# Second layer's feed-forward: gate and up by one level of Strassen in token halves of 512

## The chip, the cores and the metric

The kernel runs on one core of one Trainium2 chip. The metric is the device time of one execution in microseconds (us). Runs of this kernel lie within some 0.15% of each other.

## What is computed

A decoder trunk of two layers, for 1024 tokens and 16 meta tokens in front of them (1040), model width 1024, in float32. Each layer is a token mixer and a gated feed-forward block (SwiGLU) with 2816 hidden features; the change is in what follows the second layer's attention.

```python
for i in range(DEPTH):
    hn = rms_norm(h, mix_norm_g[i])
    ...
    h = h + swiglu(rms_norm(h, ffn_norm_g[i]), ffn_w_gate[i], ffn_w_up[i], ffn_w_down[i])
h = rms_norm(h, final_norm_g)
return h[:, N_META:]

def swiglu(h, w_gate, w_up, w_down):
    return (jax.nn.silu(h @ w_gate) * (h @ w_up)) @ w_down
```

## The kernel before

**Matrix products.** Activations lie with the features on the 128 partitions and the tokens along the free axis. Each float32 operand is split into a high part, rounded by ScalarE (a CAST in the profile), and a low part, the rest, subtracted by VectorE or GpSimd (`split_w` L153, `norm_gen` L261). A product is then three TensorE matmuls (`mm3`, L163 to L165: high by high, high by low, low by high) into one PSUM bank; the fourth, low by low, is left out.

**Tokens.** They are handled in three chunks of 348, 348 and 344; in the second layer the meta tokens are dropped, and the chunks are 332, 348 and 344 wide. The residual `h` lies in SBUF during a feed-forward block and in the DRAM tensor `hdram` during attention.

**Feed-forward** (`ffn`). The 2816 features are 22 tiles of 128, taken in 11 pairs. For each tile and chunk `phase_a` makes gate and up (8 blocks of the contraction, 24 matmuls each) in a PSUM pair `gu`; ScalarE applies SiLU (L549), VectorE multiplies (L551), and the product is split into `ah` and `al`. For each chunk `phase_b` multiplies by the pair's down weights into 8 banks `y`, which VectorE adds to `h` (L567). A pair is 2 x 3 x 48 = 288 matmuls for gate and up and 3 x 8 x 6 = 144 for down, 432 in all, of 332 to 348 columns. The weights of a tile (`raw_g`, `raw_u`, `raw_d`, 512 KB each) come by SyncE's DMA queue and are split in whole tiles, 128 x 1024.

**Around it.** The attention's output projection is made in pieces: `wo_early_gen` for the chunk of 332 during the last heads, `wo_part` and `wo_gen` for the other two, `wo_last` for the last head's share (`wot`). `wo_tail` weaves these with the three norms of the feed-forward's input, `norm_gen` (squares on ScalarE, sums `acc_f` on GpSimd, two small matmuls for the statistics, then `xt_f`, `xh_f`, `xl_f` for each of 8 blocks). The last pair is woven with the final norm (`final` in `run`), and its last chunk (332 tokens) is in hand-written order. Elsewhere a scheduler orders each engine's instructions from the program's order and its estimates.

## Time and profile before

| | us |
|---|---|
| three runs | 2196.35, 2196.79, 2199.15 (median 2196.79) |
| the profiled execution, its own time | 2194.79 |
| its span | 2193.0 |
| TensorE busy | 2158.8 |
| VectorE, ScalarE, GpSimd busy | 1065.3, 726.0, 354.8 |

PE is TensorE, DVE VectorE, ACT ScalarE, POOL GpSimd, SP SyncE, whose queue issues all DMAs. The profile gives for each group of instructions its busy time, its mean duration and what ended the idle time of its engine just before. Matmul durations overlap in it; the distance between two starts is what one costs in a row. PEclk is the granted clock of TensorE, 1.00 for 2.4 GHz and 0.50 for 1.2 GHz.

### The profile page before, as it was taken

How to read it: one execution, taken by the hardware profiler on the slowest of the kernel's cores; microseconds unless marked ns; L12 is line 12 of the kernel's file. 1: busy time of each engine (PE TensorE's matmuls, PEld its weight loads, DVE VectorE, ACT ScalarE, POOL GpSimd, SP SyncE). 2: the span in 40 equal slices, each digit the busy share in tenths (PEclk: the TensorE clock that was granted, in tenths of full speed). 3: DMA queues.
4: the chain of work that ended last, by engine and by line, in shares of the span. 5: the costliest groups of instructions: out<-in, count | busy, mean ns of one | idle time of the engine just before them, and what ended most of it. 6: DMA issues, size and time to landing. Idle time of an engine off the chain costs nothing.

```text
span 2193.0 us, 33618 instructions
## 1 busy us (share of the span) xinstructions
PE 2158.8 (98%) x13978; PEld 2141.7 (98%) x13978; DVE 1065.3 (49%) x2000; ACT 726.0 (33%) x1509; POOL 354.8 (16%) x542
## 2 busy tenths in 40 slices
PE   8999999999999999999999999999999999999998
PEld 7999999999999999999999999999999999999998
DVE  6653334343343446777666677464343333333335
ACT  5531211112111134666666655242112211112114
POOL 4300000000000025444444333230000000000004
PEclk8999999999999999999999999999999999999998
DMA  7011101011110112111111147212011111111002
...
DMA packets 49363, 137.02 MB, mean 62 GB/s; under 512 B 5346, under 2 KB 20491, under 8 KB 48699
## 3 DMA queue, kind: packets, MB, share of 16 engines
...
q14 instruction: 43, 0.35, 0.0%
...
## 4 chain that ended last, share of the span: by engine, by line
PE 92%; DVE 3%; ACT 3%; DMA 1%; issue 1%; POOL 0%; SPq 0%; DVEq 0%; ACTq 0%; POOLq 0%
PE gu L163 15%; PE gu L164 15%; PE gu L165 15%; PE y L163 7%; PE y L164 7%; PE y L165 7%; PE pj L165 4%; PE pj L163 4%; PE pj L164 4%; PE o L880 2%; PE s L800 2%; PE o L885 1%; PE at L863 1%; PE s L798 1%; PE pl L353 1%; DVE xt_f L258 1%
## 5 line engine op out<-in xcount | busy, mean ns | idle before, releaser
L567 DVE TENSOR_TENSOR h<-h,y 128x348 f32<-128x348 f32 (+2 forms) x520 | 263.0, 511 | 315.3 <-PE y L165 315.1
L549 ACT ACTIVATE s<-gu 128x348 f32<-128x348 f32 (+1 forms) x132 | 60.2, 456 | 831.3 <-PE gu L165 831.2
L163 PE MATMUL y<-ah,d_h 128*128 128x348 f32 (+2 forms) x1008 | 321.6, 321 | 3.8 <-DVE h L567 3.6
L164 PE MATMUL y<-al,d_h 128*128 128x348 f32 (+2 forms) x1008 | 322.4, 320 | 0.0
L165 PE MATMUL y<-ah,d_l 128*128 128x348 f32 (+2 forms) x1008 | 322.4, 320 | 0.0
L164 PE MATMUL gu<-xl_f,u_h 128*128 128x348 f32 (+2 forms) x1008 | 321.9, 319 | 0.0
L164 PE MATMUL gu<-xl_f,g_h 128*128 128x348 f32 (+2 forms) x1008 | 321.7, 319 | 0.0
L165 PE MATMUL gu<-xh_f,u_l 128*128 128x348 f32 (+2 forms) x1008 | 321.6, 319 | 0.1
L163 PE MATMUL gu<-xh_f,g_h 128*128 128x348 f32 (+2 forms) x1008 | 321.7, 319 | 0.0
L165 PE MATMUL gu<-xh_f,g_l 128*128 128x348 f32 (+2 forms) x1008 | 321.6, 319 | 0.0
L163 PE MATMUL gu<-xh_f,u_h 128*128 128x348 f32 (+2 forms) x1008 | 321.5, 319 | 0.0
L551 DVE TENSOR_TENSOR s<-gu,s 128x348 f32<-128x348 f32 (+1 forms) x132 | 67.9, 514 | 346.1 <-ACT s L549 346.1
L163 PEld LDWEIGHTS y<-ah,d_h 128*128 128x128 f32 x1008 | 190.0, 189 | 5.7 <-DVE h L567 5.3
L164 PEld LDWEIGHTS y<-al,d_h 128*128 128x128 f32 x1008 | 190.6, 189 | 0.0
L165 PEld LDWEIGHTS y<-ah,d_l 128*128 128x128 f32 x1008 | 190.1, 189 | 0.0
L164 PEld LDWEIGHTS gu<-xl_f,g_h 128*128 128x128 f32 x1008 | 189.5, 188 | 0.6 <-issue 0.6
L165 PEld LDWEIGHTS gu<-xh_f,u_l 128*128 128x128 f32 x1008 | 189.6, 188 | 0.3 <-DVE u_l L153 0.3
L163 PEld LDWEIGHTS gu<-xh_f,g_h 128*128 128x128 f32 x1008 | 189.6, 188 | 0.0
L165 PEld LDWEIGHTS gu<-xh_f,g_l 128*128 128x128 f32 x1008 | 189.6, 188 | 0.0
L163 PEld LDWEIGHTS gu<-xh_f,u_h 128*128 128x128 f32 x1008 | 189.6, 188 | 0.0
L164 PEld LDWEIGHTS gu<-xl_f,u_h 128*128 128x128 f32 x1008 | 189.5, 188 | 0.0
L163 PE MATMUL pj<-xh_m,w_h 128*128 128x348 f32 (+2 forms) x576 | 187.9, 326 | 0.9 <-DVE oo L922 0.9
...
## 6 DMA issues: line engine op xcount, KB each, us to landing
...
```

The lines of the kernel that those rows point to most:

```text
L163: nc.tensor.matmul(out, wh, xh, start=first, stop=False)
L164: nc.tensor.matmul(out, wh, xl, start=False, stop=False)
L165: nc.tensor.matmul(out, wl, xh, start=False, stop=last)
L258: nc.vector.scalar_tensor_tensor(t[:, :w], h[:, k, a:b], self.gcol(g, k), r[:, :w], op0=ALU.mult, op1=ALU.mult)
L353: yield lambda x=x, i=i: self.nc.tensor.matmul(ps[:, a:b], x[:r, j, k * P : k * P + P], rhs, start=start and i == 0, stop=stop and i == 1)
L549: nc.scalar.activation(st[:, :w], ps[:, 0, :w], AF.Silu)
L551: nc.vector.tensor_tensor(at[:, :w], ps[:, 1, :w], st[:, :w], op=ALU.mult)
L567: nc.vector.tensor_tensor(h[:, m, a:b], h[:, m, a:b], ps[:, :w], op=ALU.add)
L798: nc.tensor.matmul(out, qz[m], s["kl"][:, ka:kb], start=False, stop=True)
L800: nc.tensor.matmul(out, s["qs", m][:, qsl], s["kd", m][:, ka:kb], start=True, stop=False)
L863: nc.tensor.transpose(pt[:rows, j, :], a[:, kb * KB : kb * KB + rows], self.ident)
L880: nc.tensor.matmul(po[:, : 2 * P], ah[:rows, kb, :], s["vhl"][:rows, kb, :], start=j == 0, stop=j == nl)
```

## The change

`layer1` takes the place of `wo_tail` and of the second layer's `ffn`. Tokens are handled in two halves of 512, and `h` becomes one tile `H` (128 x 8 x 1024). The first and the last pair of features are computed as before, but 512 columns wide (the last chunks 512, 256, 256). For the nine pairs between (`wino`), gate and up are 2 x 2 block products: a pair's two feature tiles by two token halves, with the contraction of 1024 in two halves. Winograd's form of Strassen's scheme does each with seven products instead of eight.

- The four sums of weight blocks S1 to S4 (tiles `z`) are made by GpSimd for each pair and projection (`sub`, 8 instructions a pair). The sums of token blocks T1 to T4 are made once (`twist_gen`): VectorE and GpSimd add and subtract the split parts, and the sums are split anew. T4 takes the place of a block of x and is turned back before the last pair.
- Each product has 12 matmuls of 512 columns. Its weights are a `unit`, split from 128 x 512 by ScalarE and VectorE into one of five buffers (`ring`).
- Products 6, 4 and 5 are added in PSUM onto banks that hold earlier ones, and between these ScalarE copies a bank out (`hold`) and VectorE adds another to the copy (`put`).
- `down_gen` multiplies the pair before by its down weights, 96 matmuls of 512 columns.

A Strassen pair thus has 2 x 84 + 96 = 264 matmuls of 512 columns. Beside them stand 14 splits of units, 8 holds, 8 puts, 4 SiLU, 4 multiplications, 4 splits of activations, 4 splits of down weights and 16 additions to `H`.

```diff
...
+HALF = 512
+OFF1 = {1: 0, 2: 512, 0: 768}
+W1 = {1: 512, 2: 256, 0: 256}
+NT = 6
+NRING = 5
...
+    def wo_last(self, ox, wr):
...
+                self.mm3(ps, ww, [self.part8(ox, hl, NH - 2 + j) for hl in range(2)], j == js[0], j == 1)
+            nc.vector.tensor_tensor(h[:, m, :], h[:, m, :], ps, op=ALU.add)
...
+    def split(self, src, hi, lo, eng=None):
+        self.nc.scalar.copy(hi, src)
+        (eng or self.nc.vector).tensor_tensor(lo, src, hi.bitcast(F32), op=ALU.subtract)
+
+    def unit(self, src, nm, pool=None, tag="u", eng=None, f2=False):
+        t = (pool or self.ring).tile([P, 2, HALF], F32R, tag=tag, name=nm)
+        hi, lo = t[:, 0, :], t[:, 1, :]
+        if f2:
+            self.split(src, *(v.rearrange("p (f n) -> p f n", f=2) for v in (hi, lo)), eng)
+        else:
+            self.split(src, hi, lo, eng)
+        return hi, lo
+
...
+        def diff(nm, a, b, op=ALU.subtract):
+            d, e = self.tt(f"{nm}d"), self.tt(f"{nm}e")
+            V.tensor_tensor(d, a[0], b[0], op=op)
+            G.tensor_tensor(e, a[1], b[1], op=op)
+            V.tensor_tensor(d, d, e, op=ALU.add)
+            return d
+
+        def less(nm, a, b):
+            d = self.tt(f"{nm}d")
+            V.tensor_tensor(d, a[0], b, op=ALU.subtract)
+            V.tensor_tensor(d, d, a[1], op=ALU.add)
+            return d
+
...
+        def pair(n, k):
+            return [self.T[n, hl, k] for hl in range(2)]
+
+        for k in range(4):
+            b11, b12, b21, b22 = ([part(j, i, hl, k) for hl in range(2)] for i in range(2) for j in range(2))
+            t3 = diff(f"t3_{k}", b22, b12)
+            self.split(t3, *pair(3, k), G)
+            t1 = diff(f"t1_{k}", b12, b11)
+            self.split(t1, *pair(1, k), G)
+            t2 = less(f"t2_{k}", b22, t1)
+            self.split(t2, *pair(2, k), V)
+            yield
+        yield True
+        for k in range(4):
+            t4 = diff(f"t4_{k}", [part(0, 1, hl, k) for hl in range(2)], [t.bitcast(F32) for t in pair(2, k)])
+            self.split(t4, *pair(4, k), V)
+        yield True
+        for k in range(4):
+            b12 = diff(f"b12_{k}", [part(0, 0, hl, k) for hl in range(2)], [t.bitcast(F32) for t in pair(1, k)], ALU.add)
+            self.split(b12, *pair(4, k), G)
+
...
+    def wino(self, p, nm, src, x, use):
+        nc, ap = self.nc, self.ap
+        V, G = nc.vector, nc.gpsimd
+        held = {}
+
+        def hold(i, j, b):
+            if nm == "u" and i == j == 1:
+                t = self.actp.tile([P, HALF], F32, tag="ex", name=f"c{nm}_{p}_{i}{j}")
+            else:
+                t = self.tt(f"c{nm}_{p}_{i}{j}")
+            held[i, j] = t
+            nc.scalar.copy(t, b)
+
+        def put(i, j, b):
+            t = held.pop((i, j))
+            V.tensor_tensor(t, t, b, op=ALU.add)
+            use(i, j, t)
+
+        raw = self.raw2([ap[src][FT + 2 * p + i] for i in range(2)], f"raw_{nm}_{p}")
+        A = {(i + 1, k + 1): raw[:, i, k * HALF : k * HALF + HALF] for i in range(2) for k in range(2)}
+        S = dict(enumerate(self.z, 1))
+
+        def sub(o, a, b, op=ALU.subtract):
+            G.tensor_tensor(S[o], a, b, op=op)
+
+        xw = self.psa(f"xw_{nm}_{p}")
+        X, W = xw[:, 0, :], xw[:, 1, :]
+
+        def mul(out, n, a, b, start=True):
+            hi, lo = self.unit(a, f"w{n}_{nm}_{p}")
+            for k in range(4):
+                ww = [t[:, k * P : k * P + P] for t in (hi, lo)]
+                self.mm3(out, ww, [b(hl, k) for hl in range(2)], start and k == 0, k == 3, skip=not start)
+
+        def bx(i, j):
+            return lambda hl, k: self.part8(x[j], hl, 4 * i + k)
+
+        def bt(n):
+            return lambda hl, k: self.T[n, hl, k]
+
+        sub(3, A[1, 1], A[2, 1])
+        sub(1, A[2, 1], A[2, 2], ALU.add)
+        mul(X, 1, A[1, 1], bx(0, 0))
+        yield
+        Y = self.psb(f"y2_{nm}_{p}")
+        mul(Y, 2, A[1, 2], bx(1, 0))
+        hold(0, 0, Y)
+        put(0, 0, X)
+        yield
+        mul(W, 7, S[3], bt(3))
+        hold(1, 1, W)
+        sub(2, S[1], A[1, 1])
+        sub(4, A[1, 2], S[2])
+        yield
+        mul(X, 6, S[2], bt(2), False)
+        yield
+        mul(W, 4, A[2, 2], bt(4), False)
+        hold(1, 0, W)
+        put(1, 0, X)
+        yield
+        Z = self.psb(f"y3_{nm}_{p}")
+        mul(Z, 3, S[4], bx(1, 1))
+        hold(0, 1, Z)
+        yield
+        mul(X, 5, S[1], bt(1), False)
+        put(0, 1, X)
+        put(1, 1, X)
+        yield
+
...
+    def down_gen(self, p, a):
+        raw = self.down_raw(p)
+        for q in range(4):
+            u = self.down_unit(p, raw, q)
+            for e in range(2):
+                m = 2 * q + e
+                for lo in (0, HALF):
+                    ps = self.psb(f"yd_{p}_{m}_{lo}")
+                    self.down_mm(ps, u, e, a, lo, HALF, (0, 1), True, True)
+                    self.down_add(m, lo, HALF, ps)
+                yield
+
...
+    def layer1(self, ox, ws, part):
+        nc, tc, ap = self.nc, self.tc, self.ap
+        NP = FT // 2
+        with ExitStack() as right, ExitStack() as left:
+            with tc.using_default_side("right"):
+                hp = right.enter_context(tc.tile_pool(name="hp", bufs=1, reuse_waits="tile"))
+                self.tmp = right.enter_context(tc.tile_pool(name="tmp", bufs=NT, reuse_waits="tile"))
+            self.H = H = hp.tile([P, KT, 2 * HALF], F32, name="H")
+            self.hh = [H[:, :, j * HALF : j * HALF + HALF] for j in range(2)]
+            for j in range(2):
+                nc.sync.dma_start(self.hh[j], self.hdram[:, :, N_META + j * HALF : N_META + j * HALF + HALF])
...
+            drain(self.wo_last(ox[0], wr))
+            n0 = self.norm_half(0, "ffn1", "f10", x)
+            drain(self.wo_gen(list(range(4, KT)) + list(range(4)), ox[1], ws, part), n0)
+            self.wk.close()
+            self.rawp = left.enter_context(tc.tile_pool(name="rawp", bufs=2, reuse_waits="tile"))
+            self.ring = left.enter_context(tc.tile_pool(name="ring", bufs=NRING, reuse_waits="tile"))
+            self.actp = left.enter_context(tc.tile_pool(name="actp", bufs=1, reuse_waits="tile"))
+            self.z = [self.actp.tile([P, HALF], F32, tag=f"z{i}", name=f"z{i}") for i in range(4)]
+            a = self.new_a(0)
+            n1 = self.norm_half(1, "ffn1", "f11", x)
+
+            def plain(j):
+                for s in range(2):
+                    gu = self.gu_units(s, f"c{s}{j}")
+                    yield from self.plain_up(s, x, j * HALF, HALF, gu, s, a)
+
+            drain(plain(0), n1)
+            tqx = ExitStack()
+            self.tq = tqx.enter_context(tc.tile_pool(name="tq", bufs=1, reuse_waits="tile"))
+            tw = self.twist_gen(x)
+            run = plain(1)
+            while not next(tw):
+                fill(run, 8)
+            drain(run)
+            next(tw)
+            for p in range(1, NP - 1):
+                s = {}
+                drain(self.gate_gen(p, x, s))
+                drain(self.down_gen(p - 1, a))
+                a = self.new_a(p)
+                drain(self.up_gen(p, x, s, a))
+            p = NP - 1
+            drain(tw)
+            tqx.close()
+            late = left.enter_context(tc.tile_pool(name="late", bufs=1, reuse_waits="tile"))
+            self.tp = left.enter_context(tc.tile_pool(name="tpl", bufs=2, reuse_waits="tile"))
+            self.tw = HALF
+            prev, a = a, self.new_a(p)
+            gu = [self.gu_units(2 * p, "e0"), None]
+            aa = lambda s, c: self.plain_up(2 * p + s, x, OFF1[c], W1[c], gu[s], s, a)
+            down = self.down_gen(p - 1, prev)
+            drain(aa(0, 1))
+            drain(down)
...
+            with tc.manual_schedule(engines=ORD):
+                drain(self.final(0, self.down_last(p, us, a, OFF1[0], W1[0])))
...
-            for c in (1, 0, 2):
-            xn1, side = self.wo_tail(ox, ws, part, tail)
...
-            self.ffn(1, xn1, tail, final, lambda n: side if n == 1 else iter(()), cs=(1, 2, 0), closing=closing)
+        self.layer1(ox, ws, part)```

Three places show what the order of the instructions becomes; `_49` is the end of a semaphore's name. The first is SyncE's queue during the last head of the attention. Before, the `h` of the chunk of 348 (`h_1_1`) is loaded among the DMAs of `wo_early_gen` (`hx`, `raw_woe`):

```order
L954 DMA hdram_82<-hx_1_13369 128x332 [waits DMAHW4_49,DVE_49]
L944 DMA hx_7_13927<-hdram_82 128x332 [waits DMAHW5_49,DMAHW4_49]
L1204 DMA h1_1_14173<-hdram_82 128x2784 [waits DMAHW6_49,PE_49]
L137 DMA raw_woe_7_13921<-in_wo_dram 128x1024 [waits DMAHW7_49,DMAHW0_49,Pool_49]
L954 DMA hdram_82<-hx_2_13433 128x332 [waits DVE_49]
```

After, both halves of `H` are loaded behind them, and the first load waits for semaphores of PE and POOL, which the last head's transposes and its last multiplication (`o`, L898 of before) raise, because `H` takes the memory of attention tiles:

```order
L941 DMA hdram_82<-hx_7_1_13956 128x256 [waits DMAHW4_49,DMAHW2_49,DVE_49]
L144 DMA raw_wo_2_14222<-in_wo_dram 128x1024 [waits DMAHW0_49,DVE_49]
L144 DMA raw_wo_3_14228<-in_wo_dram 128x1024 [waits DMAHW3_49,DVE_49]
L1370 DMA H_14197<-hdram_82 128x8x512 [waits DMAHW2_49,DMAHW6_49,DMAHW1_49,DMAHW7_49,PE_49,Pool_49]
L1370 DMA H_14197<-hdram_82 128x8x512
```

The load has moved behind the last work of the attention. What PE has there beside it is the last head's share `wot`, groups of 3 or 6 matmuls, each of which VectorE adds to `H`.

The second place is VectorE in the second part of `twist_gen`, during pair 0; it has no counterpart before. `t2_3d` to `t4_3d` are sums for T2 and T4, `T21` is T2's low part (T4's is written into `x_f11_1`), `yd_0_m_lo` are down results of pair 0, and `d_0_1` is the second unit of its down weights:

```order
L1111 TENSOR_TENSOR T21_14718<-t2_3d_14930,T20_14717 128x512 [waits Activation_49]
L1300 TENSOR_TENSOR H_14197<-H_14197,yd_0_0_512_15108 128x512 [waits PE_49]
L1137 TENSOR_TENSOR t4_2d_14949<-x_f10_2_14436,T20_14717 128x512 [waits DVE_49]
L1137 TENSOR_TENSOR t4_3d_14956<-x_f10_2_14436,T20_14717 128x512 [waits DVE_49]
L1111 TENSOR_TENSOR x_f11_1_14644<-t4_0d_14935,x_f11_0_14643 128x512 [waits Activation_49]
L1300 TENSOR_TENSOR H_14197<-H_14197,yd_0_1_0_15116 128x512 [waits PE_49]
L1139 TENSOR_TENSOR t4_1d_14942<-t4_1d_14942,t4_1e_14943 128x512 [waits Pool_49]
L1300 TENSOR_TENSOR H_14197<-H_14197,yd_0_1_512_15124 128x512 [waits PE_49]
L1111 TENSOR_TENSOR d_0_1_15132<-raw_d_0_15094,d_0_1_15132 128x512 [waits Activation_49]
```

The split of `d_0_1`, for which PE waits at its product `yd_0_2`, stands behind 70 rows that begin with the norm of the second half. GpSimd's queue up to the same point (`t1_3e`, `t4_0e` are its halves of the same sums, `z` the sums S of the next projections, `T31`, `T11` low parts):

```order
L1138 TENSOR_TENSOR t1_3e_14924<-x_f11_1_14644,x_f10_1_14435 128x512 [waits DVE_49,Pool_49]
L1224 TENSOR_TENSOR z2_14495<-raw_u_1_15239 128x512 [waits DMAHW4_49,DMAHW3_49]
L1224 TENSOR_TENSOR z0_14493<-raw_u_1_15239 128x512 [waits DVE_49]
L1111 TENSOR_TENSOR T31_14716<-t3_3d_14916,x_f11_2_14645 128x512 [waits Activation_49]
L1138 TENSOR_TENSOR t4_0e_14936<-x_f10_1_14435,T21_14718 128x512 [waits DVE_49]
L1224 TENSOR_TENSOR z1_14494<-z0_14493,raw_u_1_15239 128x512 [waits Pool_49]
L1111 TENSOR_TENSOR T11_14720<-t1_3d_14923,T10_14719 128x512 [waits Activation_49]
L1138 TENSOR_TENSOR t4_1e_14943<-x_f10_1_14435,T21_14718 128x512 [waits Pool_49]
```

VectorE's third row from the end adds GpSimd's last one here, `t4_1e`, so GpSimd's queue stands ahead of `d_0_1` too, 29 rows from the norm on.

The third place is VectorE in the middle of the block. Before, in pair 5 (`s` is SiLU times up, `al` the low part, `g1`, `d1` the weights of a tile):

```order
L551 TENSOR_TENSOR s_1_10_0_17807<-gu_1_10_0_17758,s_1_10_0_17807 128x332 [waits Activation_49]
L153 TENSOR_TENSOR d1_12_l_18207<-raw_d1_12_18204,d1_12_h_18206 128x1024 [waits DMAHW6_49,Activation_49]
L555 TENSOR_TENSOR al_1_10_0_17811<-s_1_10_0_17807,ah_1_10_0_17810 128x332 [waits Activation_49]
L551 TENSOR_TENSOR s_1_11_1_17881<-gu_1_11_1_17832,s_1_11_1_17881 128x348 [waits Activation_49]
L555 TENSOR_TENSOR al_1_11_1_17885<-s_1_11_1_17881,ah_1_11_1_17884 128x348 [waits Activation_49]
L551 TENSOR_TENSOR s_1_11_2_17937<-gu_1_11_2_17888,s_1_11_2_17937 128x344 [waits Activation_49]
L555 TENSOR_TENSOR al_1_11_2_17941<-s_1_11_2_17937,ah_1_11_2_17940 128x344 [waits Activation_49]
L153 TENSOR_TENSOR g1_13_l_18381<-raw_g1_13_18378,g1_13_h_18380 128x1024 [waits DMAHW7_49,PE_49,Activation_49]
```

After, in a Strassen pair (`w3_u_3` is the unit of product 3 of up of pair 3; `cu`, `cg` are the held copies: a row that adds `xw` is a `put`, one that reads `cg` the multiplication):

```order
L1111 TENSOR_TENSOR w3_u_3_16168<-z3_14496,w3_u_3_16168 128x512 [waits Activation_49]
L1216 TENSOR_TENSOR cu_3_00_16106<-cu_3_00_16106,xw_u_3_16072 128x512 [waits Activation_49]
L1111 TENSOR_TENSOR w5_u_3_16185<-z0_14493,w5_u_3_16185 128x512 [waits PE_49,Activation_49]
L1282 TENSOR_TENSOR cu_3_00_16106<-cu_3_00_16106,cg_3_00_15830 128x512 [waits DVE_49]
L1111 TENSOR_TENSOR w1_g_4_16214<-raw_g_4_16208,w1_g_4_16214 128x512 [waits DMAHW1_49,Activation_49]
L1111 TENSOR_TENSOR al_3_16068<-cu_3_00_16106,ah_3_16067 128x512 [waits Activation_49]
L1111 TENSOR_TENSOR w2_g_4_16230<-raw_g_4_16208,w2_g_4_16230 128x512 [waits PE_49,Activation_49]
L1111 TENSOR_TENSOR w7_g_4_16249<-z2_14495,w7_g_4_16249 128x512 [waits Activation_49]
L1111 TENSOR_TENSOR w6_g_4_16268<-z1_14494,w6_g_4_16268 128x512 [waits Activation_49]
L1216 TENSOR_TENSOR cu_3_10_16161<-cu_3_10_16161,xw_u_3_16072 128x512 [waits Activation_49]
```

The rows are all 128 x 512 now, and between splits of units stand rows that add PSUM banks to copies which ScalarE has made.

## Rows read from the trace of the kernel before

**Rows 1.** The page's first lines, and its chain that ended last by engine.

```profile
span 2193.0 us, 33618 instructions
...
PE 2158.8 (98%) x13978; PEld 2141.7 (98%) x13978; DVE 1065.3 (49%) x2000; ACT 726.0 (33%) x1509; POOL 354.8 (16%) x542
...
PE 92%; DVE 3%; ACT 3%; DMA 1%; issue 1%; POOL 0%; SPq 0%; DVEq 0%; ACTq 0%; POOLq 0%
```

**Rows 2.** Windows: length, PE, PEld, DVE, ACT, POOL busy us, granted clock, DMA.

```profile
1500.00:2100.00 600.00, 600.00 (x3851) 600.00 (x3850) 222.96 (x374) 105.47 (x164) 0.00 (x0) 1.00 0.16 49
1329.00:1331.00 2.00, 2.00 (x9) 2.00 (x9) 2.00 (x5) 1.33 (x4) 0.78 (x1) 0.50 0.68 202
```

**Rows 3.** Timeline of SP's queue: two loads of down weights, seven pairs apart.

```profile
1524.02 0.33 SPq L137 DMA_DIRECT2D raw_d<-in_down_dram  x1
...
1995.41 0.33 SPq L137 DMA_DIRECT2D raw_d<-in_down_dram  x1
```

**Rows 4.** Timeline of PE, 512 columns in the attention: start, duration.

```profile
1347.93 0.40 PE L800 MATMUL s<-qk,qk 128*128 128x512 f32 x1
...
1348.86 0.31 PE L163 MATMUL woe<-ox,woe_h 128*128 128x332 f32 x1
```

**Rows 5.** Timeline of PE, 332 columns in the last pair's down products.

```profile
2171.65 0.32 PE L163 MATMUL y<-ah,d_h 128*128 128x332 f32 x1
...
2178.49 0.33 PE L163 MATMUL y<-ah,d_h 128*128 128x332 f32 x1
```

**Rows 6.** Groups by line and shape: ScalarE, VectorE, GpSimd; busy us, mean ns.

```profile
L867 ACT CAST ath<-at 116x512 fp32r<-116x512 f32 x64 | 36.8, 591 | 1.7 <-PE at L863 1.1
...
L567 DVE TENSOR_TENSOR h<-h,y 128x348 f32<-128x348 f32 x264 | 133.5, 514 | 153.9 <-PE y L165 153.9
...
L153 DVE TENSOR_TENSOR d_l<-raw_d,d_h 128x1024 fp32r<-128x1024 f32 x42 | 52.1, 1240 | 22.1 <-ACT d_h L149 22.1
...
L868 DVE TENSOR_TENSOR atl<-at,ath 116x512 fp32r<-116x512 f32 x64 | 43.5, 684 | 29.9 <-ACT ath L867 29.7
...
L153 POOL TENSOR_TENSOR w_l<-raw_w,w_h 128x256 fp32r<-128x256 f32 x84 | 60.4, 748 | 32.2 <-ACT w_h L149 28.8 <-issue 2.8
...
L153 POOL TENSOR_TENSOR woe_l<-raw_woe,woe_h 128x1024 fp32r<-128x1024 f32 x4 | 9.6, 2390 | 5.9 <-ACT woe_h L149 5.8
...
L1229 POOL TENSOR_TENSOR h<-h,acc_fin 128x332 f32<-128x332 f32 x3 | 3.1, 1056 | 5.6 <-ACT acc_fin L239 5.6
```

**Rows 7.** Timeline of DVE around 1425 and 1437 us.

```profile
1423.36 0.51 DVE L261 TENSOR_TENSOR xl_f<-xt_f,xh_f 128x348 fp32r<-128x348 f32 x1
1423.79 2.43 DVE L258 SCALAR_TENSOR_TENSOR xt_f<-h,vec,acc_f 128x348 f32<-128x348 f32 x2
...
1437.60 1.57 DVE L153 TENSOR_TENSOR u_l<-raw_u,u_h 128x1024 fp32r<-128x1024 f32 x1 [2.88 <-ACT u_h L149]
1439.10 1.91 DVE L153 TENSOR_TENSOR d_l<-raw_d,d_h 128x1024 fp32r<-128x1024 f32 x1
```

**Rows 8.** Timeline of POOL at the same times.

```profile
1423.41 1.26 POOL L192 TENSOR_TENSOR acc_f<-acc_f,sq_f 128x344 f32<-128x344 f32 x1 [0.35 <-ACT sq_f L181]
1424.62 1.22 POOL L261 TENSOR_TENSOR xl_f<-xt_f,xh_f 128x348 fp32r<-128x348 f32 x1
...
1435.21 7.51 POOL L192 TENSOR_TENSOR acc_f<-acc_f,sq_f 128x332 f32<-128x332 f32 x6
```

**Rows 9.** Timelines of DVE and POOL where DVE reads PSUM.

```profile
1427.63 1.31 DVE L1084 TENSOR_TENSOR h<-h,wot 128x332 f32<-128x332 f32 x3
...
1428.44 5.84 POOL L192 TENSOR_TENSOR acc_f<-acc_f,sq_f 128x344 f32<-128x344 f32 x5 [2.60 <-ACT sq_f L181]
```

**Rows 10.** DMA issues: count, KB each, median us from issue to landing.

```profile
h<-hdram SPq DMA_DIRECT2D x2, 1392.0 KB, 5.9
...
ox<-odram SPq DMA_DIRECT2D x2, 1204.0 KB, 13.1
```

**Rows 11.** Timeline of PE: the last down product.

```profile
2178.82 0.31 PE L165 MATMUL y<-ah,d_l 128*128 128x332 f32 x1
```

More of the change, by code (lines that the diff above doesn't have):

```diff
@@ new lines, in new_a, with gate_gen, use, up_gen @@
+    def new_a(self, p):
+        return [self.actp.tile([P, 2, 2 * HALF], F32R, tag=f"a{i}", name=f"a{i}_{p}") for i in "hl"]
+    def gate_gen(self, p, x, s):
+        def use(i, j, t):
+            s[i, j] = t
+            self.nc.scalar.activation(t, t, AF.Silu)
+        yield from self.wino(p, "g", "gate", x, use)
+    def up_gen(self, p, x, s, a):
+        def use(i, j, t):
+            self.nc.vector.tensor_tensor(t, t, s.pop((i, j)), op=ALU.mult)
+            self.split(t, *(v[:, i, j * HALF : j * HALF + HALF] for v in a))
+        yield from self.wino(p, "u", "up", x, use)
@@ new lines, in down_raw, with down_unit, down_mm @@
+    def down_raw(self, p):
+        return self.raw2([self.ap["down"][FT + 2 * p + i] for i in range(2)], f"raw_d_{p}")
+    def down_unit(self, p, raw, q, pool=None, tag="u"):
+        return self.unit(raw[:, :, 2 * q * P : 2 * q * P + 2 * P], f"d_{p}_{q}", pool, tag, f2=True)
+    def down_mm(self, ps, u, e, a, lo, w, fs, first, last):
+        for i in fs:
+            ww = [t[:, i * 2 * P + e * P : i * 2 * P + e * P + P] for t in u]
+            self.mm3(ps, ww, [t[:, i, lo : lo + w] for t in a], first and i == fs[0], last and i == fs[-1])
```

334 lines of the change are left out of this document (204 added, 130 removed).

## The prediction

> **What bounds the kernel now.** I read the page's sums and chain first: TensorE is busy for 2158.8 us of 2193.0, and the chain that ended last lies on it for 92% [rows 1]. Then the windows by stage: in the 600 us from 1500, the second layer's feed-forward, TensorE never pauses, its clock is at 1.00 (2.4 GHz), VectorE is busy for 223 us, ScalarE for 105, GpSimd not at all [rows 2]. So work taken from TensorE there shortens the kernel one for one, and the other engines have room, as long as nothing that they newly do stands in front of a matmul. The timelines give what one matmul costs in a row, and the groups by shape what the other engines' instructions cost.
>
> **A pair before.** Two loads of down weights seven pairs apart were issued at 1524.02 and 1995.41 [rows 3]: 471.4 / 7 = 67.34 us a pair, for 432 matmuls 0.1559 each, at 341 columns in the mean.
>
> **A matmul of 512 columns.** Nothing in the feed-forward has this width, but the attention does: four in a row from 1347.93 to 1348.86, 0.2325 each [rows 4]. From the other side: 45 matmuls of 332 columns took 2171.65 to 2178.49, 0.152 each [rows 5]; with the pair's mean that is (0.1559 - 0.152) / 9.3 = 0.00042 a column, and 0.152 + 180 x 0.00042 = 0.2276 at 512. I take 0.230; the bounds are 0.2265 and 0.2325, and over some 3,050 matmuls of this width they are worth -10 and +8 us.
>
> **Strassen pairs.** 2 x 84 + 96 = 264 matmuls x 0.230 = 60.7 us instead of 67.34: 6.6 a pair, 59.8 us for nine. Pair 0 has 288 wide matmuls, 66.2 us, 1.1 less. The output projection has 384 instead of 576: 88.3 against 89.8, 1.5 less. The last pair, half of it in pieces of 256, stays within 0.1. After the last down product at 2178.82 [rows 11] 14 us follow to the end of the span; five dependent steps there (addition, square, scaling, multiplication, store) handle 256 columns instead of 332. GpSimd's multiplication of 332 is 1.06 us and its 256 is 0.75 [rows 6], so about 0.3 a step, 1.5 us together (bounds 0 and 3). **Saved: 63.9 us.**
>
> **What the other engines do in a pair.** VectorE: 14 + 8 + 4 + 4 + 4 + 16 = 50 instructions of 512 columns. One lasts 0.684 [rows 6]; three additions of 332 in a row take 1.31 [rows 9], 0.07 less each than the single 0.51, so 0.61 in a row, 30.5 us of 60.7. ScalarE: 34 x 0.59 [rows 6] = 20 us. GpSimd: 8 x 1.30 (between 0.748 at 256 and 2.390 at 1024 [rows 6]) = 10.4 us. All fit. Where each bank is handed over, a copy (0.59) and an addition (0.61) stand between two products on the same bank, 1.3 us with the hand-overs, and the order puts at least one product of another bank there, 12 matmuls or 2.8 us. That is the cover; where it is gone, a pair loses up to eight times 1.3. GpSimd's four weight sums depend on one another, 5.2 us, and slow VectorE while they run (next part). I take 0.3 us a pair, 3 us together, bounds 0 and 12.
>
> **VectorE beside GpSimd.** In the steady stage before, GpSimd is idle [rows 2], so the price of both together is read from the norms. At 1423.79 two scalings take 2.43 us on VectorE beside two GpSimd instructions of 1.26 and 1.22 [rows 7, 8]; at 1437.60 and 1439.10 two weight splits take 1.57 and 1.91 instead of 1.24 [rows 6 to 8]. In the first place, from 1423.36 to 1426.22, VectorE did three instructions of 0.51 [rows 6] and GpSimd two of 0.93 (from its prices at 256 and 1024), 3.39 in turn, in 2.86 us: 0.84. In the second VectorE's 2.48 lie in 3.41, and GpSimd's six instructions take 7.51 instead of 5.6 [rows 8], so it did some 1.5 in these 3.41: 0.86. So with operands in SBUF the two nearly take turns: together they need 0.85 of the sum. Additions that read PSUM are not slowed: three take 1.31 beside GpSimd [rows 9]. The Trainium skill (SBUF — State Buffer, section "SBUF: two separate sides") goes further: the port pair that the two share is an exclusive lock, so that of a VectorE instruction with two SBUF inputs and a GpSimd one the later waits for the whole of the other. The trace agrees in kind, but 0.85 stands where the rule gives 1; by the rule the next part's 65 us would be 77 and the whole 2180. This is a rule against the change, and a rival below.
>
> **The sums of tokens.** They are made while TensorE does the second half of pair 0. VectorE's queue from the start of the second half's norm to the split of the down unit `d_0_1`, for which `yd_0_2` waits, is 71 instructions, 64 of them with SBUF operands alone; GpSimd's, which the third last of these needs, is 29. TensorE has 171 matmuls there, 39.3 us; the statistics' copy takes 1.2 of these, which leaves 38. VectorE alone needs 71 x 0.61 = 43.3, a stall of 5. Shared: 64 x 0.61 = 39.0 and 29 x 1.30 = 37.7, together 76.7 x 0.85 = 65.2, the seven others beside GpSimd: **a stall of 27 us**, in several pieces (weight units and down units that come late). I take it, as this chain is nearest to the rows that were measured; bounds 5 and 38. What is late next, the T4 sums behind `d_0_1`, falls on products 30 matmuls later and costs no more. After 1.6 us of idle time TensorE's clock was 0.50 from 1329 to 1331 [rows 2]; each such piece would cost 1 us more, which I leave to the range.
>
> **The norm of the first half** shares the two engines with the splits of pair 0's weights in the same manner, for a shorter time: 2 us (0 to 5). The turning back of T4 lies beside 60 matmuls, 13.8 us, and is hidden; the last pair's splits, 1 us.
>
> **The load of `H`** moves behind the attention. Two DMAs of 2048 KB: at 1392 KB in 5.9 us [rows 10] the first lands in 8.7 us; if both share the queues as the loads of 1204 KB did (13.1 [rows 10]), later. Beside it TensorE has 30 matmuls, 6.9 us, before the fifth group of `wot` needs a bank that only an addition to `H` frees. I take 3 us, bounds 2 and 10. Behind that load on SyncE stand the first weights of pair 0, needed 40 us later, which are hidden.
>
> **The sum**, against the profiled execution's own 2194.8: -63.9 + 3 + 2 + 27 + 3 + 1 = -27.9, so 2166.9. The median of the runs lies 2.0 above that execution: 2168.9, say 2168.
>
> **Rivals.**
> - *Hidden sums.* VectorE and GpSimd do not hold each other up with these operands; the stall is VectorE's own 5 us: 22 less, 2146. Against it stand the rows at 1423 and 1437.
> - *Strict turns.* Each waits for the other's whole instruction: 76.7 - 38 = 39, 12 us more, 2180; with 0.2325 a matmul 2187. For it speaks that 0.84 to 0.86 is near 1.
> - *Stalls in every pair (the other side).* The hand-over of a bank, copy, addition, next product, stands in front of TensorE, since VectorE's queue is in order and a `put` waits behind splits for units that wait for GpSimd's sums. From 28 / 9 = 3.1 us a pair more than I count, the change gains nothing; uncovered, 8 x 1.3 = 10.4 a pair, 2168 + 9 x 10.1 = 2259. Against it: VectorE is free for half of each pair.
> - *No saving by width.* If 512 columns cost 67.34 / 264 = 0.255 in this stage, the pairs save nothing and the time is about 2228. Against it: 0.2325 in the attention.
>
> **Chances.** Forecast 0.54 (own range 2158 to 2176), hidden sums 0.22, strict turns 0.16, stalls in every pair 0.05, no saving 0.03. The range reaches from the hidden sums with a matmul of 0.2265 (2138) to the strict turns at the upper price (2187). A change of 0.2%, 4.4 us, is what can be told from none. Faster: the first three and a third of the stalls, 0.93; within 0.2%: 0.01; slower: 0.06.
>
> **What would show it.** Right: down loads of the middle pairs 60 to 62 us apart; 512-column matmuls 0.228 to 0.232 apart; TensorE idle for some 25 us between the norm of the second half and the end of pair 1's gate, ended by VectorE, with VectorE and GpSimd instructions there at 0.8 to 1.5 and 1.5 to 2 us; a gap of 2 to 4 us before `wot`'s fifth group, ended by an addition that waited for the load. Wrong: pairs 64 us or more apart, with idle time ended by `put` rows; or no idle time beside the sums.

## The result and the profile after

The changed kernel takes 2171.61 us (median of four runs, 2170.14 to 2175.12) against 2197.48 for the kernel before: a ratio of 0.9884, 95% interval 0.9867 to 0.9901. The forecast was 2168, with a range of 2138 to 2187. The profiled execution took 2170.14, its span is 2168.3.

The page's first lines and the chain by engine, for [rows 1]:

```profile
span 2168.3 us, 30456 instructions
...
PE 2101.5 (97%) x12150; PEld 1950.8 (90%) x12150; DVE 1250.5 (58%) x2115; ACT 811.3 (37%) x1668; POOL 507.5 (23%) x626
...
PE 89%; DVE 5%; ACT 3%; issue 1%; DMA 1%; POOL 1%; SPq 0%; DVEq 0%; ACTq 0%; POOLq 0%
```

TensorE is busy for 57 us less, the span is only 25 us shorter: it now idles for 66.8 us where it idled for 34.2. Windows of the changed kernel, with the columns of [rows 2]: length, busy time of PE, PEld, DVE, ACT, POOL, granted clock, DMA.

```profile
1450.00:1490.00 40.00, 30.50 (x122) 23.38 (x121) 39.96 (x35) 14.96 (x25) 30.77 (x18) 0.96 0.17 53
1490.00:1530.00 40.00, 23.55 (x69) 16.76 (x70) 38.82 (x44) 12.73 (x22) 26.46 (x15) 0.70 0.08 27
1600.00:2000.00 400.00, 400.00 (x1767) 331.20 (x1766) 256.89 (x334) 131.76 (x227) 83.85 (x53) 1.00 0.16 53
2130.00:2155.00 25.00, 17.41 (x123) 16.41 (x123) 14.54 (x27) 9.18 (x22) 11.09 (x13) 0.86 0.36 127
```

The third row is the Strassen pairs' stage: TensorE never pauses, VectorE is busy for 64% and GpSimd for 21%. The loss stands in the other rows. From 1450 to 1530, around the token sums, 191 matmuls that need 43.3 us at 0.2267 each take 80: 36.7 us are lost. TensorE is idle for 26.0 of them; in the other 10.7 its work is slower: 31 matmuls start 0.43 us apart (the clock's lower level), some 6 us, and the rest stands at the edges of ten pauses. VectorE is busy for 78.8 of the 80 us. From 2130 to 2155, in the last pair, TensorE is idle for another 7.6 us, at a mean clock of 0.86; nine matmuls of 256 columns start 0.21 apart there instead of 0.12, some 1.4 us more.

Two loads of up weights, six pairs apart, for [rows 3]:

```profile
1634.26 0.80 SPq L1125 DMA_DIRECT2D raw_u<-in_up_dram  x2
...
1993.30 0.80 SPq L1125 DMA_DIRECT2D raw_u<-in_up_dram  x2
```

359.04 / 6 = 59.84 us a pair, 0.2267 a matmul.

What TensorE waited for between 1385 and 1560 (view of waits: total us, times, longest):

```profile
PE yd L170 <- ACT d L1110: 5.8, 2, 5.0
PE yd L172 <- DVE d L1111: 5.1, 1, 5.1
PE gu L172 <- DVE c L1111: 4.1, 2, 3.0
PE xw_g L170 <- DVE s L1182: 3.7, 1, 3.7
PE gu L171 <- DVE x_f L1106: 3.7, 2, 2.8
PE yd L170 <- DVE H L1300: 3.6, 1, 3.6
PE wot L170 <- DVE H L1064: 2.4, 1, 2.4
PE y_g L172 <- DVE w_g L1111: 0.8, 1, 0.8
```

The wait of `wot` is the load of `H`, and of the two for `x_f`, low parts of the norms, the shorter one, 0.9 us at 1428, belongs to the first half's norm. All the others, 25.9 us, end with rows that stand among the token sums and the second half's norm in VectorE's or ScalarE's queue: down units (`d`), units of pairs 0 and 1 (`c`, `w_g`), the multiplication `s`, the second half's `x_f`, the addition to `H` that frees a bank. Timelines of VectorE and, under the dots, of GpSimd in that stretch, for [rows 7, 8]:

```profile
1464.89 1.78 DVE L1137 TENSOR_TENSOR t_0d<-x_f,x_f 128x512 f32<-128x512 f32 x1
1466.60 1.78 DVE L1111 TENSOR_TENSOR c<-raw_c,c 128x512 fp32r<-128x512 f32 x1
1468.30 1.74 DVE L1139 TENSOR_TENSOR t_0d<-t_0d,t_0e 128x512 f32<-128x512 f32 x1
1469.96 0.68 DVE L1111 TENSOR_TENSOR al<-s,ah 128x512 fp32r<-128x512 f32 x1
...
1464.38 3.44 POOL L1224 TENSOR_TENSOR z<-raw_g 128x512 f32<-128x512 f32 x2
1467.79 1.71 POOL L1138 TENSOR_TENSOR t_0e<-x_f,x_f 128x512 f32<-128x512 f32 x1
```

Read the starts: 1464.89, 1466.60, 1468.30, 1469.96. An addition of two SBUF operands starts every 1.70 us while GpSimd works, one of VectorE's for one of GpSimd's, and the first one after GpSimd's instruction has ended lasts 0.68, and the next starts 0.61 later. Alone, VectorE needs 0.61 in a row and GpSimd 1.29 (the shortest of its weight sums in the steady stage): 1.90 in turn, 1.70 together. The rhythm does not always hold. At 1494.12 one GpSimd instruction lasts 5.47 us while VectorE goes on at a start every 0.60 (two of VectorE's rows, seven starts apart, and GpSimd's):

```profile
1494.16 0.68 DVE L1111 TENSOR_TENSOR w_g<-z,w_g 128x512 fp32r<-128x512 f32 x1
...
1498.37 0.68 DVE L1182 TENSOR_TENSOR s<-gu,s 128x512 f32<-128x512 f32 x1
...
1494.12 5.47 POOL L1111 TENSOR_TENSOR T<-t_2d,x_f 128x512 fp32r<-128x512 f32 x1 [4.04 <-ACT x_f L1110]
```

The stretch that the prediction summed up runs in VectorE's queue from the first row of the second half's norm, at 1450.01, to the end of the split of `d_0_1`, at 1526.04. These are its windows, in the columns of [rows 2], in the changed kernel and in two runs of the next section: e8, which leaves this stretch as it is, and e2, where all token sums are on VectorE:

```profile
1450.01:1526.04 76.03, 50.07 (x174) 36.84 (x173) 74.81 (x72) 25.84 (x44) 57.23 (x32) 0.82 0.13 42
...
1455.45:1531.35 75.90, 51.98 (x174) 37.80 (x173) 75.87 (x72) 25.82 (x44) 54.00 (x32) 0.82 0.13 42
...
1454.52:1519.35 64.83, 47.93 (x174) 35.17 (x173) 64.72 (x87) 25.54 (x43) 22.57 (x12) 0.87 0.15 49
```

VectorE stands for 1.2 us of the 76.0 in the first and for none in the second, so its queue, slowed by GpSimd, sets the length of the stretch. The 173 matmuls that start in it need 39.2 us at 0.2267, which leaves 36.8: the whole loss. TensorE works 1.9 us longer in e8, and the stretch is no longer for it.

The wait for `H` and the end of the kernel, TensorE and VectorE:

```profile
1398.12 0.51 PE L170 MATMUL wot<-ox,wor 128*128 128x512 f32 x1 [2.37 <-DVE H L1064]
...
1397.38 4.88 DVE L1064 TENSOR_TENSOR H<-H,wot 128x512 f32<-128x512 f32 x8 [6.88 <-DMA H<-hdram]
```

```profile
2131.65 6.15 DVE L1354 SCALAR_TENSOR_TENSOR H<-H,vec,acc_fin 128x512 f32<-128x512 f32 x6 [2.11 <-ACT acc_fin L246]
2137.72 1.40 DVE L1300 TENSOR_TENSOR H<-H,yd 128x256 f32<-128x256 f32 x4
...
2141.96 1.11 PE L217 MATMUL ms_fin<-ones,acc_fin 128*116 128x1 f32 x6 [3.70 <-POOL acc_fin L199]
2144.62 1.20 PE L245 MATMUL mr_fin<-ident,st_fin 116*128 116x116 f32 x4 [1.56 <-DVE st_fin L241]
```

The load of `H` was issued at 1388.84; the first addition came at 1397.38 and TensorE had stood for 2.37 us. In the last pair six scalings of the first 512 tokens take 6.15 us, then come four additions of the second chunk, then the norm's statistics (`ms_fin`, `mr_fin`), for which TensorE waits 3.70 and 1.56 us.

### The profile page after: what moved, and what is told of

The parts are those of the page before. It is cut to its first block, busy times and chain, and to the rows that moved or that the text cites. A ratio compares the mean times of both kernels' runs of the same rounds, so it can differ in the third digit from the quotient of the medians.

```text
span 2168.3 us, 30456 instructions
## 1 busy us (share of the span) xinstructions
PE 2101.5 (97%) x12150; PEld 1950.8 (90%) x12150; DVE 1250.5 (58%) x2115; ACT 811.3 (37%) x1668; POOL 507.5 (23%) x626
## 3 DMA queue, kind: packets, MB, share of 16 engines
q8 instruction: 95, 1.56, 0.3%
## 4 chain that ended last, share of the span: by engine, by line
PE 89%; DVE 5%; ACT 3%; issue 1%; DMA 1%; POOL 1%; SPq 0%; DVEq 0%; ACTq 0%; POOLq 0%
PE gu L171 8%; PE gu L170 8%; PE gu L172 8%; PE pj L172 4%; PE pj L170 4%; PE pj L171 4%; PE y L170 4%; PE y L171 4%; PE y L172 4%; PE yd L170 3%; PE yd L172 3%; PE yd L171 3%; PE o L860 2%; PE xw_u L170 2%; PE xw_u L172 2%; PE xw_u L171 2%
## 5 line engine op out<-in xcount | busy, mean ns | idle before, releaser
L170 PE MATMUL pj<-xh_m,w_h 128*128 128x348 f32 (+2 forms) x576 | 188.0, 326 | 1.0 <-DVE oo L896 1.0
L172 PE MATMUL pj<-xh_m,w_l 128*128 128x348 f32 (+2 forms) x576 | 185.5, 322 | 0.0
L171 PE MATMUL pj<-xl_m,w_h 128*128 128x348 f32 (+2 forms) x576 | 184.2, 320 | 0.0
L1300 DVE TENSOR_TENSOR H<-H,yd 128x512 f32<-128x512 f32 (+1 forms) x184 | 120.4, 662 | 90.3 <-PE yd L172 89.2
L199 POOL TENSOR_TENSOR acc_m<-sq_m,sq_m 128x348 f32<-128x348 f32 (+1 forms) x3 | 2.8, 932 | 672.6 <-ACT sq_m L188 672.6
L170 PE MATMUL y<-ah,d_h 128*128 128x348 f32 (+1 forms) x480 | 153.9, 321 | 3.8 <-DVE h L574 3.7
L170 PE MATMUL gu<-xh_f,g_h 128*128 128x348 f32 (+1 forms) x480 | 153.9, 321 | 0.0
L170 PE MATMUL gu<-xh_f,u_h 128*128 128x348 f32 (+1 forms) x480 | 153.9, 321 | 0.0
L171 PE MATMUL gu<-xl_f,g_h 128*128 128x348 f32 (+1 forms) x480 | 153.8, 320 | 0.0
L171 PE MATMUL gu<-xl_f,u_h 128*128 128x348 f32 (+1 forms) x480 | 153.8, 320 | 0.0
L172 PE MATMUL gu<-xh_f,g_l 128*128 128x348 f32 (+1 forms) x480 | 153.6, 320 | 0.0
L171 PE MATMUL y<-al,d_h 128*128 128x348 f32 (+1 forms) x480 | 153.6, 320 | 0.0
L170 PE MATMUL yd<-ah,d 128*128 128x512 f32 (+1 forms) x368 | 142.2, 389 | 11.8 <-ACT d L1110 5.8
L172 PE MATMUL gu<-xh_f,u_l 128*128 128x348 f32 (+1 forms) x480 | 153.5, 320 | 0.0
L172 PE MATMUL y<-ah,d_l 128*128 128x348 f32 (+1 forms) x480 | 153.4, 320 | 0.0
L172 PE MATMUL yd<-ah,d 128*128 128x512 f32 (+1 forms) x368 | 140.3, 386 | 5.1 <-DVE d L1111 5.1
L171 PE MATMUL yd<-al,d 128*128 128x512 f32 (+1 forms) x368 | 142.0, 386 | 0.5 <-DVE al L1111 0.5
L170 PEld LDWEIGHTS pj<-xh_m,w_h 128*128 128x128 f32 x576 | 108.5, 188 | 1.8 <-DVE oo L896 1.3
L171 PEld LDWEIGHTS pj<-xl_m,w_h 128*128 128x128 f32 x576 | 108.6, 189 | 0.5
```

The source lines that it names most:

```text
L170: nc.tensor.matmul(out, wh, xh, start=first, stop=False, skip_group_check=skip)
L171: nc.tensor.matmul(out, wh, xl, start=False, stop=False, skip_group_check=skip)
L172: nc.tensor.matmul(out, wl, xh, start=False, stop=last, skip_group_check=skip)
L199: eng.tensor_tensor(acc[:, :w], x[:, :w], sq[:, :w], op=ALU.add)
L1300: self.nc.vector.tensor_tensor(h, h, ps, op=ALU.add)
```

## The experiments

Executions of one program differ by 0.8 to 8.5 us in these rounds (the kernel before ran from 2191.83 to 2200.37 in one of them, 0.4% and not 0.15%), and in the profiled ones the end of the attention alone moves: the last head's transposes (`ot`) start between 1385.6 and 1391.8 in the traces below. So beside each time I give two stages of its trace: from these transposes to the issue of pair 9's down load (the middle), and from there to the end of the span. The ratios go by the kernel before as it ran in the same round (medians 2195.0 to 2197.9). The changed kernel, e4, e5 and e8 have the same middle, and their traces give 642.4 to 644.0 for it; the changed kernel, e1, e2, e4, e6 and e10 have the same end, 136.7 to 138.2. So 1.6 us more or less in one stage of one trace say nothing.

| kernel | time, median | ratio to before, 95% interval | middle | end |
|---|---|---|---|---|
| changed | 2171.61 | 0.9867 to 0.9901 | 642.4 | 138.2 |
| e1 two plain pairs | 2156.89 | 0.9808 to 0.9840 | 628.7 | 138.1 |
| e2 sums on VectorE | 2163.69 | 0.9839 to 0.9871 | 634.3 | 136.9 |
| e3 all plain | 2184.97 | 0.9939 to 0.9971 | | |
| e4 scalings later | 2170.75 | 0.9872 to 0.9910 | 643.7 | 137.5 |
| e5 last chunk 512 | 2170.56 | 0.9861 to 0.9888 | 644.0 | 136.6 |
| e6 two plain, sums on VectorE | 2150.55 | 0.9772 to 0.9799 | 623.2 | 136.7 |
| e7 e6, last chunk 512 | 2151.10 | 0.9778 to 0.9805 | 624.0 | 135.7 |
| e8 without scalings | 2170.34 | 0.9858 to 0.9885 | 644.0 | 134.8 |
| e9 e6, last chunk 332 | 2154.65 | 0.9794 to 0.9822 | 624.5 | 139.4 |
| e10 e6, norm on VectorE | 2151.88 | 0.9785 to 0.9812 | 624.5 | 136.8 |

**What Strassen brings, and what it costs (e3).** The pairs' loop of `layer1` without `wino` and `twist_gen`:

```diff
...
-                drain(self.gate_gen(p, x, s))
                 drain(self.down_gen(p - 1, a))
                 a = self.new_a(p)
-                drain(self.up_gen(p, x, s, a))
+                for s in range(2):
+                    gu = self.gu_units(2 * p + s, f"c{p}{s}")
+                    for j in range(2):
+                        drain(self.plain_up(2 * p + s, x, j * HALF, HALF, gu, s, a))
```

> No Strassen pair: all eleven pairs as eight-product blocks in halves of 512, without token sums or weight sums; everything around stays as in the changed kernel. Theory (the change gains 2.0 us a pair by the width alone and 5.5 us more by the seventh product, and loses 33 us by the token sums): 2171.6 + 9 x 5.45 - 33 = about 2188 us, 9 faster than before. Rival (the seventh product brings little, the wider matmuls most): about 2150.

It took 2184.97, near the theory and far from the rival's 2150. The three longest sums of its waits in the second layer:

```profile
PE ms_fin L217 <- POOL acc_fin L199: 4.4, 2, 3.7
PE gu L171 <- DVE x_f L1106: 3.7, 2, 2.8
PE wot L170 <- DVE H L1064: 2.2, 1, 2.2
```

Beside the norms' own 3.7 us, which the changed kernel has too, there is no wait where the token sums stood. Of the 3.7, 0.9 belong to the first half and 2.8 to the second, so the changed kernel lost 36.7 - 2.8 = 33.9 us there beyond the norm, and this accounts for the difference: a pair takes 65.28 us here, 5.44 more, and 2170.1 + 9 x 5.44 - 33.9 = 2185. The width of 512 alone, with the loss at the end in it, is worth some 10 us (0.9955); the seventh product saves 49 more and its sums take 34 of them back. The last pair's waits are those of the changed kernel (4.4 for `ms_fin` in both), so that loss has nothing to do with Strassen.

**Which engine the sums are on (e2).** In `twist_gen` GpSimd's share goes to VectorE:

```diff
-        V, G = nc.vector, nc.gpsimd
+        V, G = nc.vector, nc.vector
```

> All of GpSimd's additions and low parts for the token sums are given to VectorE; the weight sums stay on GpSimd. Theory (the two engines nearly take turns on operands in SBUF, both together needing 0.85 of the sum): VectorE's queue to the down unit d_0_1 is 86 instructions instead of 71, GpSimd's 14 instead of 29, (79 x 0.61 + 14 x 1.3) x 0.85 = 56 us instead of 65, and the stall shrinks by 8 to 10: about 2161 us, though VectorE has more to do. Rival (GpSimd's work runs freely beside VectorE's, which is simply too long): 15 x 0.61 = 9 us more, about 2180.

It took 2163.69, near the theory's 2161 and far from the rival's 2180. That is 7.9 us below the changed kernel, and 7.1 below e4, which ran in the same round and hardly differs from it (see below). The middle is 8.1 us shorter, and the stretch to the split of `d_0_1` fell from 76.0 to 64.8 (the theory said 65 to 56), though VectorE has 15 instructions more to do in it, 28 in the whole kernel (2143 against 2115). VectorE's timeline in the stretch where GpSimd is idle now:

```profile
1480.06 0.68 DVE L1137 TENSOR_TENSOR t_1d<-x_f,x_f 128x512 f32<-128x512 f32 x1
1480.66 0.68 DVE L1111 TENSOR_TENSOR c<-raw_c,c 128x512 fp32r<-128x512 f32 x1
1481.26 0.68 DVE L1111 TENSOR_TENSOR T<-t_0d,x_f 128x512 fp32r<-128x512 f32 x1
```

Every 0.60 us where it was 1.70. This is what tells turns from running side by side: work taken from GpSimd and given to VectorE, whose queue sets the length of this stretch, made the kernel faster. Of two SBUF operands, GpSimd's 1.29 us cost VectorE 1.09; VectorE does the same work in 0.60.

**More plain work beside the sums (e1).** Pair 1 is computed plainly too; `second` stands for the second half of pair 0, its down products and both halves of pair 1, and these are woven with the sums:

```diff
...
-            run = plain(1)
+            run = second()
             while not next(tw):
-                fill(run, 8)
+                fill(run, 14)
             drain(run)
+            a = a1[0]
             next(tw)
-            for p in range(1, NP - 1):
+            for p in range(2, NP - 1):
```

> Pair 1 too is computed plainly, so that eight pairs are Strassen pairs and the token sums T1 to T3 lie beside one and a half pairs of plain matmuls instead of half a pair. Theory (the 26 us of idle time and some 7 us at the lower clock between 1450 and 1530 us come from VectorE and GpSimd being too slow for that one window): the pair costs 288 x 0.2267 = 65.3 instead of 59.8 us, 5.5 more, and nearly all of the 33 us goes away: about 2144 us. Rival (the waits come from the start of the Strassen pairs themselves, their ring of five units and GpSimd's weight sums): the gap stays, only later, and the time is about 2177.

It took 2156.89, between what the theory and the rival say. The middle is 13.7 us shorter, with 5.5 paid for the plain pair: 19 of the 34 us are gone, not all. What is left of the waits up to 1640:

```profile
PE gu L170 <- ACT c L1110: 4.5, 1, 4.5
PE gu L172 <- DVE c L1111: 3.8, 3, 1.9
PE gu L171 <- DVE x_f L1106: 3.7, 2, 2.8
...
PE xw_g L170 <- DVE cg L1216: 1.3, 1, 1.3
```

The Strassen pairs' start waits for 1.3 us only, so the rival falls; but the first sums still stand beside the norm and in front of pair 0's units (`c`).

**Both together (e6).** e1 with e2's edit, and the second half of pair 0 placed ahead of the first sums:

```diff
...
             run = second()
+            fill(run, 16)
             while not next(tw):
-                fill(run, 14)
+                fill(run, 9)
```

> Two plain pairs, all token sums on VectorE, and the first of them placed only after the second half of pair 0. Theory (what the run with two plain pairs still lost, 13 us of idle time from 1450 to 1500 and some 3 at the lower clock, is VectorE and GpSimd taking turns where the first sums lie beside the norm): GpSimd is left with the norm's four low parts there, and 8 to 11 us of it go away: about 2147 us, 5 of them being the plain pair's price. Rival (the norm of the second half alone makes TensorE wait): about 2156 as with two plain pairs.

2150.55, 0.9786 of the kernel before and clearly below the changed kernel; it lies between the theory's 2147 and the rival's 2156. The longest waits left in its middle:

```profile
PE yd L172 <- DVE d L1111: 4.3, 1, 4.3
PE gu L171 <- DVE x_f L1106: 3.7, 2, 2.8
```

These are the norms' 3.7, and 4.3 for a down unit behind T4's sums. 623.2 stands against 642.4 - 33.9 + 5.5 = 614.0 for a middle without any loss by the sums, so some 9 us of that loss remain, 5.2 of them waits. **e10** gives the norms' low parts to VectorE as well:

```diff
-            eng = nc.gpsimd if k % 2 else nc.vector
+            eng = nc.vector
             eng.tensor_tensor(xl, t, xh.bitcast(F32), op=ALU.subtract)
```

> The kernel with two plain pairs and all token sums on VectorE, and now the norms' low parts too are VectorE's alone; only the weight sums, the norms' square sums and the final norm are left to GpSimd. Theory (beside GpSimd an instruction with SBUF operands takes 1.70 us for what the two need 0.61 and 1.29 for): four low parts at 0.61 instead of 1.7 shorten the chain from the statistics to the second half's first products, and some 2 to 3 of the 3.7 us of waits there go away: about 2148 us. Rival (the chain is VectorE's own work, now 4 instructions longer): 2151 to 2153.

2151.88, no gain: the waits for the norms' parts (`x_f`) fell from 3.7 to 2.7 us, less than forecast, and the middle did not shrink. The time is the rival's, but 1 us is less than these runs can tell, so what sets the norm's chain stays open.

**The end of the kernel (e4, e8, e5, e9).** e4 wanted the scalings behind the additions by the order of the program:

```diff
-            drain(aa(1, 2), self.final(1))
+            f1 = self.final(1)
+            for _ in aa(1, 2):
+                fill(f1, 3)
             drain(self.down_chunk(p, us, a, OFF1[2], W1[2]))
-            drain(aa(1, 0), self.final(2))
+            drain(aa(1, 0), self.final(2), f1)
```

> In the last pair the scaling of the final norm of the first 512 tokens is put behind the additions of the second chunk's down products. Theory (TensorE's 7.6 us of idle time and the lower clock from 2138 to 2155 us begin with these additions, which stand behind six scalings of 512 columns, 6.2 us, in VectorE's queue): about 6 us less, 2165 us. Rival (the chain through squares, GpSimd's sums and the statistics is itself too long for a chunk of 256): no change, 2171, or the scaling comes later and the end with it, up to 2175.

2170.75, but it does not test the theory: the scheduler put the scalings where they were, as VectorE's timeline shows.

```profile
2136.48 6.14 DVE L1354 SCALAR_TENSOR_TENSOR H<-H,vec,acc_fin 128x512 f32<-128x512 f32 x6 [2.12 <-ACT acc_fin L246]
2142.55 1.40 DVE L1300 TENSOR_TENSOR H<-H,yd 128x256 f32<-128x256 f32 x4
```

e8 takes them out (`elif c != 1:` in `final`), which leaves the first 512 tokens' outputs partly unscaled.

> The changed kernel without VectorE's six final scalings of the first 512 tokens (left out altogether; those outputs stay unscaled). Theory (the idle time from 2138 on begins because the second chunk's last four additions stand behind these 6.2 us of scalings): the additions come some 3 to 4 us earlier, and so does the chain behind them, 6 us less in all with the clock that no longer falls: about 2165 us. Rival (the chain of squares, GpSimd's sums and statistics is too long for a last chunk of 256 in any case): 1 to 2 us less, 2170.

By the whole time, 2170.34, it cannot be told; the end's length, 134.8, is 2 to 3.4 us below the 136.7 to 138.2 of the traces with the same end. VectorE's addition, and the waits of the last pair:

```profile
2137.25 0.42 DVE L1300 TENSOR_TENSOR H<-H,yd 128x256 f32<-128x256 f32 x1 [2.40 <-PE yd L172]
...
PE mr_fin L245 <- DVE st_fin L241: 2.4, 1, 2.4
PE yd L170 <- DVE H L1300: 1.8, 1, 1.8
...
PE ms_fin L217 <- POOL acc_fin L199: 0.7, 1, 0.7
```

The additions now follow the products, and the wait of 3.70 for `ms_fin` is gone (the 0.7 that is left stands behind the last product, in the changed kernel too); but 4.7 of the 7.6 us of waits ahead of that product stay. So both hold: 2 to 3 us by the scalings in front, and 2.9 (2.4 for `mr_fin` and 0.5) by the chain of squares, sums and statistics, which is longer than a last chunk of 256. The other 1.8 (`yd` for `H`) are again scalings, those of the second chunk, which stand in front of the last chunk's additions. No run leaves these out; in e6's trace the wait does not occur, with an end of 136.7. e5 changes the widths of the three chunks:

```diff
-OFF1 = {1: 0, 2: 512, 0: 768}
-W1 = {1: 512, 2: 256, 0: 256}
+OFF1 = {1: 0, 2: 256, 0: 512}
+W1 = {1: 256, 2: 256, 0: 512}
```

> The changed kernel with the last pair's chunks 256, 256 and 512 wide instead of 512, 256, 256. Theory (in the end the second chunk's additions stand behind six scalings of the first chunk, 6.2 us at 512 columns, and the last chunk's matmuls, 256 wide, are too short to cover the norm's chain): the scalings take half, the last chunk's gate and up cover 11 us, and the 7.6 us of idle time and 2 to 3 us at the lower clock go away; after the last product everything handles 512 columns instead of 256, some 4 us more: about 2165 us. Rival (the idle time is the chain's length and comes with any width): 2171 + 4 = 2175.

2170.56, no difference. The waits did fall, as the theory has it (view of waits, last pair; the 0.4 for `ms_fin` stands behind the last product):

```profile
PE mr_fin L245 <- DVE st_fin L241: 1.3, 1, 1.3
...
PE ms_fin L217 <- POOL acc_fin L199: 0.4, 1, 0.4
PE yd L170 <- DVE H L1300: 0.4, 1, 0.4
```

but from the last product, at 2149.45, to the end of its span it is 20 us, where the changed kernel needs 13.2: the 4 us that I had put down for the wider end are nearly 7, and they eat the gain. **e7** is e6 with these widths:

> Two plain pairs, the sums on VectorE, and the last pair's chunks 256, 256, 512 wide. Theory: both gains add up, about 2141 us, faster than both kernels by clearly more than the runs differ. Rival (the end grows by as much as the idle time falls): 2147.

2151.10, the same as e6: the rival's number is the nearer one. **e9** is e6 with `OFF1 = {1: 0, 2: 512, 0: 692}` and `W1 = {1: 512, 2: 180, 0: 332}`:

> The kernel with two plain pairs and all sums on VectorE, its last pair's chunks 512, 180 and 332 wide, so that the last chunk is as wide as it was before the change. Theory (the last chunk's gate and up, 48 matmuls, must cover the norm's chain of the chunk ahead, and 332 columns cover 7.3 us, 256 only 5.8): the 6.5 us of idle time at the end fall by half and the end is 1 us longer, about 2147 us. Rival (the same sum as with 512 columns: what is gained ahead of the last product is lost behind it): 2150.

2154.65, worse than both predicted; its end is 2.7 us longer than e6's. The theory's part came true: TensorE's idle time before the last product fell from 6.1 to 3.8 us, and what follows that product is 1.7 us longer. What neither saw is the narrow chunk. TensorE's timeline, 180 columns in e9 and 256 in the changed kernel:

```profile
2103.28 0.28 PE L170 MATMUL yd<-ah,d 128*128 128x180 f32 x1
...
2104.51 0.27 PE L172 MATMUL yd<-ah,d 128*128 128x180 f32 x1
...
2149.17 0.28 PE L170 MATMUL yd<-ah,d 128*128 128x256 f32 x1
...
2150.84 0.28 PE L172 MATMUL yd<-ah,d 128*128 128x256 f32 x1
```

Eleven steps in 1.23 us are 0.112 each, fourteen in 1.67 are 0.119: a matmul of 180 columns costs nearly what one of 256 does. With 0.153 at 332 against 0.120 at 256 the two chunks' 2 x 144 matmuls take 3.6 us longer, and 3.6 - 2.3 + 1.7 = 3.0 is close to the 2.7.

## Why the prediction came out right, step by step

The side and the main mechanism were right: the pairs save, and VectorE and GpSimd hold each other up at the token sums. That the time was met to 0.2% is luck. The saving came out 8.4 us larger than forecast and the small terms 6.8 smaller; the token sums cost 9.7 more, and the end, counted as a gain alone, costs 9.0 ahead of it.

- **A matmul of 512 columns** was put at 0.230 and measured 0.2267, next to the lower bound; the line through the feed-forward's own widths had given 0.2276, and the attention's 0.2325 was the worse guide. The step "Saved: 63.9 us" was really 72: nine pairs at 7.5 us, pair 0 2.0, the projection about 1.9 (an estimate: 156 of its matmuls at 0.2325, 228 at 0.2267), the end 0.9. (By its own figures the nine pairs' 59.8 should have been 59.6.)
- **The other engines in a Strassen pair** were given 3 us, with a rival that saw a stall in every pair. There is none: 400 us without a pause. The cover of a whole product between a copy and the next use of its bank was enough, and GpSimd's four sums, at 1.29 to 1.86 us each, lie far from where they are needed.
- **VectorE beside GpSimd**: 0.85 of the sum forecast, 1.70 / 1.90 = 0.89 measured. e2 shows the mechanism. The rule that the Trainium skill states (SBUF — State Buffer, section "SBUF: two separate sides"), a lock for the whole of an instruction, is what the one-for-one rhythm looks like; the trace agrees with it nearly, since in strict turns a pair would start every 1.90 us and 1.70 lie between two starts. Additions that read PSUM are not slowed, as in [rows 9]: the one to `H` at 1518.13 lasts 0.67 beside GpSimd.
- **The sums of tokens** were put at a stall of 27 us, and 36.7 were lost. The mechanism held, but the sum made VectorE's queue to the split of `d_0_1` too short: 65.2 us, where it took 76.0. With 0.89 for 0.85, with the 32 GpSimd instructions that ran in this stretch instead of 29, and with VectorE's 8 rows that the sum left beside GpSimd counted in full, (72 x 0.61 + 32 x 1.29) x 0.89 gives the 76; that is a sum, and no run takes its three parts one by one. The slower clock, which I had left to the range ("each such piece would cost 1 us more"), is not a term of its own here: VectorE never stood for more than 1.2 us, so TensorE's slower matmuls fill time in which it would have waited. By its stall of 39 the rival of strict turns came nearer than the forecast, though the starts do not lie 1.90 apart; its 2180 is further off because the other terms together came out 6.2 us lower. Hidden sums, the rival with 0.22, are refuted by e2 and e3.
- **The norm of the first half** cost 0.9 instead of 2, and 1.6 us of such waits in the kernel before went away. **The load of `H`**: 2.4 forecast as 3. The last pair's splits and T4's turning back, put at 1 and 0, cost 0.5 at most: from 1530 to 2130 TensorE is idle for no more.
- **The end** was the wrong step: "five dependent steps there handle 256 columns instead of 332 ... 1.5 us together" saw only what comes behind the last product, which is indeed 0.9 us shorter. What it missed is ahead of it: the last chunk's gate and up at 256 columns no longer cover the norm of the chunk before, and scalings of 512 columns stand in front of that chunk's additions. Idle time and clock cost some 9 us.

The terms as measured: -72.3 + 2.4 + 0.9 - 1.6 + 36.7 + 0.5 + 9.0 = -24.4, against -24.65 between the two profiled executions. The executions' first stage alone moves by some us, so the closeness of the two says little.
